# Half of the K tiles of gate and up by Strassen's seven block products, with GpSimd summing the weights

## The chip, the cores and the metric

One NeuronCore of one Trainium2 chip runs the whole program. The metric is device microseconds of one execution. The kernel before took 2407.39 us, the median of 3 runs (2406.78 to 2407.83).

## The reference

The program is a network of three layers over 256 tokens of width 2048, in fp32: two hybrid layers (banded attention, gated linear attention, memory attention), and a third layer with two mixers and a feed forward. Only the feed forward of the third layer matters here:

```
h = rms_norm(x, norm_ffn_pre)                     # (256, 2048)
gate, up = split(h @ w_ffn_in, 2)                 # w_ffn_in: (2048, 2 * 5632)
x = x + rms_norm((silu(gate) * up) @ w_ffn_down, norm_ffn_post)
```

## The kernel before

Weights stay in HBM and stream through SBUF once. A tile of activations is kept as two parts, a high part in the reduced fp32r type and the rest (low); a tile of weights is split in the same way when it arrives. Each product is then three TensorE passes that add up in PSUM: high x high, high x low, low x high (lines 330 to 332). TensorE loads 128 x 128 of the activations as its stationary operand, and 512 columns of the weights stream through: one matmul.

A `Job` is one output of 256 rows by 512 columns (two row tiles t = 0, 1), summed over the K tiles in `order`. `run` cuts each job into parts of two K tiles (1024 columns: one slot of the 41 slots of 128 x 1024 fp32 in SBUF, 512 KB). Per part: one DMA from the SP queue into a slot (`do_load`), one ACT cast into the high slot (line 272) and one VectorE subtraction for the low slot (line 273, `do_split`), then 12 matmuls. `ahead(u)` issues loads up to N_RAW = 4 parts ahead of the splits, and splits as long as at most N_HL = 6 parts are split and not used up; it does this before the matmuls of unit u, so the program order on every engine is fixed when the program is built. All queues work in order.

Work beside the matmuls (evacuations, transposes, attention) is written as generators. `B.clock` is a running estimate of TensorE's time (0.427 ns a column); a generator yields a delay, and `pump`, called after each unit, steps those that are due. The `main` tiles of PSUM (two buffers of two banks) take the jobs in turn; four single banks serve transposes and the rest.

The feed forward has 11 blocks of 512 gate and 512 up columns, in groups of 4, 4 and 3. Each block is two jobs of 16 K tiles. `post_gate2` evacuates the gate (sigmoid on ACT, multiplication on VectorE, line 1533), `post_up2` multiplies the up product into it (line 1539), and the generator `hidden` (after FH = 4000 of the clock) transposes the result (four 128 x 128 transposes at a time, line 377) and splits it into high and low (lines 354 and 355). After each group the down projection runs over its 4 x 512 or 3 x 512 hidden columns as four jobs. The first block is special: it is fed while the norm before it is being finished, and its scale comes late.

Of the kernel before, what the change touches and what calls it, by code (L numbers as in the profile page):

```python
# [9 lines left out]
F32 = mybir.dt.float32  # L10
# [5 lines left out]
P = 128  # L16
# [27 lines left out]
FP = 2500  # L44
FQ = 2500
FS = 8000
FH = 4000
H1 = 10000
H2 = 7500
# [8 lines left out]
class Job:  # L58
# [8 lines left out]

    def __init__(self, kind, w, c0, cn, act, post, pre=None, order=None, k0=0, apart=None):  # L70
# [3 lines left out]
        self.apart = apart or (None, 0, 0)  # L74


class Act:
# [20 lines left out]
class Builder:  # L98
    def __init__(self, ctx, tc, a):
        self.tc, self.nc, self.a = tc, tc.nc, a  # L100
        pool = lambda name, bufs, **kw: ctx.enter_context(tc.tile_pool(name=name, bufs=bufs, **kw))
        self.const = pool("const", 1)
        self.tmp = pool("tmp", 2)
        self.small = pool("small", 4)
        self.psm = pool("psm", 2, space=bass.MemoryType.PSUM)
        self.pss = pool("pss", 4, space=bass.MemoryType.PSUM)
        self.dram = pool("dram", 1, space=bass.MemoryType.DRAM)
        self.free = list(range(N_SLOT))
        self.act = self.const.tile([P, NKT, 2, S], F32R, tag="act", name="act")
# [3 lines left out]
        self.clock = 0.0  # L113
        self.n = 0


# [4 lines left out]
    def alloc(self, n=1, dt=F32):  # L121
        tries = 0
        while len(self.free) < n:
            tries += 1
            assert self.side and tries < 1000, "out of slots"
# [67 lines left out]
        self.tokens[kind] -= 1  # L193

    def pump(self):
        due = [g for g in self.side if self.ready[g] <= self.clock]
        for gen in sorted(due, key=lambda g: self.ready[g])[:2]:
            self.step(gen)
# [14 lines left out]
    def run(self, jobs, loaded_first, split_first):  # L213
# [2 lines left out]
        parts, units = [], []  # L216
        groups = []
        for job in jobs:
            n = NKT if job.kind == "n" else min(1024 // job.cn, 4)
            name, lo, hi = job.apart  # L220
            for j, k in enumerate(range(0, len(job.order), n)):
                key = name if lo <= j < hi else None
                if not (key and groups and groups[-1][0] == key):
                    groups.append((key, []))
                groups[-1][1].append(len(parts))
                parts.append((job, job.order[k:k + n], k))
        for key, mine in groups:
            for ts in ((0,), (1,)) if key else ((0, 1),):
                for i in mine:
                    job, kts, k = parts[i]  # L230
                    units.append((job, i, ts, k == 0 and ts[0] == 0, k + len(kts) == len(job.order), mine[-1]))
        first_use, last_use = {}, {}
        for u, unit in enumerate(units):
# [2 lines left out]
        raws, hls = {}, {}  # L236
        loaded = split = 0

        def pieces(i, n):

            return [slice(k, k + 1) for k in range(n)] if i == 0 else [slice(0, n)]

        def do_load(i):
            job, kts, _ = parts[i]
            (raws[i],) = self.alloc(1)
            n, r0 = len(kts), (job.k0 + kts[0]) * P
            src = job.w[r0:r0 + n * P, job.c0:job.c0 + job.cn].rearrange("(k p) c -> p k c", p=P)
            dst = self.s(raws[i])[:, :n * job.cn].rearrange("p (k c) -> p k c", c=job.cn)
            for ks in pieces(i, n):
                self.load(dst[:, ks], src[:, ks])  # L250
            if i == 0:
                loaded_first()

        def do_split(i):
            job, kts, _ = parts[i]
            n = len(kts) * job.cn
            src = self.s(raws[i])[:, :n]
            if job.kind == "n":
                hls[i] = self.alloc(1, F32R)
                src = src.rearrange("p (k c) -> p k c", c=job.cn)  # L260
                h, l = (self.pair(hls[i], job.cn)[:, :len(kts), j, :] for j in range(2))
            else:
                hls[i] = self.alloc(2, F32R)
                h, l = (self.s(x)[:, :n] for x in hls[i])
            if i == 0:
                for k in range(len(kts)):
                    cs = slice(k * job.cn, (k + 1) * job.cn)
                    self.split_to(h[:, cs], l[:, cs], src[:, cs])
                self.release([raws.pop(i)])
                split_first()  # L270
                return
            nc.scalar.copy(h, src)  # L272
            nc.vector.tensor_tensor(l, src, h.bitcast(F32), ALU.subtract)  # L273
            self.release([raws.pop(i)])

        def room(u):

            _, i, ts, _, _, end = units[u]
            if ts != (0,):
                return len(self.free) > RESERVE  # L280
            if loaded <= end:
                return len(self.free) > 2
            coming = 2 * max(0, end + 1 - split) - sum(r <= end for r in raws)
            return len(self.free) - coming > HOLD

        def ahead(u):

            nonlocal loaded, split
            cap, nraw, reserve, far = N_HL, N_RAW, RESERVE, len(units)
            if len(units[u][2]) == 1:  # L290
                cap, reserve, far = len(parts), 0, u + NEAR
            if u < 8:
                cap, nraw = min(cap, 2 + u), min(nraw, 1 + u)
            while True:
                if loaded < len(parts) and len(raws) < nraw and room(u):
                    do_load(loaded)
                    loaded += 1
                elif split < loaded and len(hls) < cap and len(self.free) > reserve + 1 and first_use[split] <= far:
# [5 lines left out]
        for u, (job, i, ts, first, last, _) in enumerate(units):  # L304
            while split <= i:
                if loaded == split:
                    do_load(loaded)
                    loaded += 1
                do_split(split)
                split += 1  # L310
            if len(ts) == 2:
                ahead(u)
            if first:
                if job.pre:
                    job.pre()
# [5 lines left out]
            for k, kt in enumerate(kts):  # L321
# [3 lines left out]
                st, en = at + k == 0, at + k == len(job.order) - 1  # L325
                if job.kind == "x":
                    for t in ts:
                        o = job.ps[:, t, :job.cn]
                        rows = slice(t * P, t * P + P)
                        nc.tensor.matmul(o, xh[:, rows], h[:, k, :], start=st, stop=False)  # L330
                        nc.tensor.matmul(o, xh[:, rows], l[:, k, :], start=False, stop=False)  # L331
                        nc.tensor.matmul(o, xl[:, rows], h[:, k, :], start=False, stop=en)  # L332
# [13 lines left out]
            if len(ts) == 1:  # L346
                ahead(u)
            self.pump()


    def split_to(self, h, l, src, scale=None):
# [29 lines left out]
def network(ctx, tc, a):  # L381
# [76 lines left out]
    def feeder(act, t, delay, gap=1500):  # L458
        yield delay
        while act.left[t]:  # L460
            act.feed_next(t)
            yield gap


    def halves(ps):
# [96 lines left out]
    def start_late(act, *args):  # L562
        late["gen"] = late_feed(act, *args)
        B.start(late["gen"])
# [927 lines left out]
    def mix_done(ids, t):  # L1492
# [11 lines left out]
        if t == 0:  # L1504
            B.start(feeder(fact, 0, F0, FG))
        else:
            start_late(fact, [f[0], f[1]], x1res, None, lambda: B.release(ids + f["wi"]), False)

    def pre_w2():
        f["wi"] = B.alloc(2)  # L1510
# [30 lines left out]
            B.start(f[("gen", c)])  # L1541
        return post

    def hidden(c, gi):

        yield FH
        if len(f["h"]) <= 2 * c:
            f["h"] += B.alloc(2, F32R)
        for n in range(2):
# [29 lines left out]
    for g, n in enumerate((4, 4, 3)):  # L1579
        for c in range(n):  # L1580
            c0 = 512 * (at + c)
            head = (g, c) == (0, 0)
            jobs.append(Job("x", wf, c0, 512, fact, first_gate if head else post_gate2, apart=("ffn", 0, 8) if head else None))
            jobs.append(Job("x", wf, D_FF + c0, 512, fact, first_up if head else post_up2(c), apart=("ffn", 0, 4) if head else None))
        order, k0 = range(4 * n), 4 * at
# [61 lines left out]
```

## Time and profile before

| | |
|---|---|
| median of 3 runs | 2407.39 us (2406.78 to 2407.83) |
| the profiled execution | 2407.96 us, span 2406.2 us |
| TensorE (PE) busy | 2390.2 us, 12105 matmuls |
| VectorE (DVE) busy | 1476.3 us |
| ScalarE (ACT) busy | 1099.0 us |
| GpSimd (POOL) busy | 400.8 us |

The profile is one execution. PE's busy time is modelled and its matmuls overlap; the distance from one start to the next is what a matmul costs. Busy time of an engine is an average over stages; a stage is read by itself, in a window. In the views, "slot" is any of the SBUF slots, "main_j" the PSUM tile of a job, "bank" one of the single PSUM banks.

### The profile page before, as it was taken

How to read it: one execution, taken by the hardware profiler on the slowest of the kernel's cores; microseconds unless marked ns; L12 is line 12 of the kernel's file. 1: busy time of each engine (PE TensorE's matmuls, PEld its weight loads, DVE VectorE, ACT ScalarE, POOL GpSimd, SP SyncE). 2: the span in 40 equal slices, each digit the busy share in tenths (PEclk: the TensorE clock that was granted, in tenths of full speed). 3: DMA queues.
4: the chain of work that ended last, by engine and by line, in shares of the span. 5: the costliest groups of instructions: out<-in, count | busy, mean ns of one | idle time of the engine just before them, and what ended most of it. 6: DMA issues, size and time to landing. Idle time of an engine off the chain costs nothing. (4 is left out here: it accounts for less than half of the span.)

```text
span 2406.2 us, 31460 instructions
## 1 busy us (share of the span) xinstructions
PE 2390.2 (99%) x12105; PEld 2015.7 (84%) x12105; DVE 1476.3 (61%) x1671; ACT 1099.0 (46%) x1472; POOL 400.8 (17%) x601
## 2 busy tenths in 40 slices
PE   9999999999999999999999999999999999999998
PEld 8888888888888888888888888888888888888886
DVE  6587567666855667766765656657545544554455
ACT  6444445345454553655544544445434423443433
POOL 0330010004400110364764340001000000000000
PEclk9999999999999999999999999999999999999999
DMA  9646567674656674854654666675755655555653
GB/s 327 184 149 184 173 187 262 209 239 133 188 160 186 206 252 156 275 164 125 185 161 146 201 185 194 202 242 186 242 176 180 194 185 193 201 183 177 209 192 131
DMA packets 313911, 464.64 MB, mean 193 GB/s; under 512 B 21961, under 2 KB 161569, under 8 KB 313761
## 3 DMA queue, kind: packets, MB, share of 16 engines
q1 hardware_dynamic: 312528, 459.48, 60.7%
q8 instruction: 95, 1.56, 0.3%
q0 software_dynamic: 640, 2.10, 0.2%
q10 hardware_dynamic: 592, 1.06, 0.1%
q14 instruction: 56, 0.45, 0.1%
HBM read 454.18 MB, written 8.40 MB: 192 GB/s over the span
## 5 line engine op out<-in xcount | busy, mean ns | idle before, releaser
L273 DVE TENSOR_TENSOR slot<-slot,slot 128x1024 fp32r<-128x1024 f32 x810 | 1006.9, 1287 | 190.5 <-ACT slot L272 186.7
L272 ACT CAST slot<-slot 128x1024 fp32r<-128x1024 f32 x810 | 807.8, 1046 | 266.2 <-DVE slot L273 123.6
L339 PE MATMUL main_j<-act,slot 128*128 128x512 f32 x1824 | 651.0, 400 | 0.0
L330 PE MATMUL main_j<-slot,act 128*128 128x512 f32 x1608 | 636.2, 396 | 0.0
L331 PE MATMUL main_j<-slot,act 128*128 128x512 f32 x1608 | 626.4, 390 | 2.8 <-DVE slot L273 2.8
L332 PE MATMUL main_j<-slot,act 128*128 128x512 f32 x1608 | 626.8, 390 | 0.0
L340 PE MATMUL main_j<-act,slot 128*128 128x256 f32 x1824 | 509.9, 280 | 0.0
L339 PEld LDWEIGHTS main_j<-act,slot 128*128 128x128 f32 x1824 | 342.4, 188 | 80.2 <-issue 1.1
L331 PEld LDWEIGHTS main_j<-slot,act 128*128 128x128 f32 x1608 | 302.4, 188 | 63.6 <-DVE slot L273 3.8
L332 PEld LDWEIGHTS main_j<-slot,act 128*128 128x128 f32 x1608 | 301.8, 188 | 63.9
L330 PEld LDWEIGHTS main_j<-slot,act 128*128 128x128 f32 x1608 | 302.2, 188 | 61.3 <-ACT slot L272 0.5
L340 PEld LDWEIGHTS main_j<-act,slot 128*128 128x128 f32 x1824 | 344.1, 189 | 0.8
L330 PE MATMUL main_j<-slot,slot 128*128 128x512 f32 x600 | 236.1, 394 | 0.0
L332 PE MATMUL main_j<-slot,slot 128*128 128x512 f32 x600 | 233.8, 390 | 0.0
L331 PE MATMUL main_j<-slot,slot 128*128 128x512 f32 x600 | 233.6, 389 | 0.0
L447 POOL TENSOR_TENSOR rsl<-rsl,nhalf 128x1 f32<-128x1 f32 x8 | 6.2, 775 | 991.7 <-DVE rsl L446 991.7
L332 PEld LDWEIGHTS main_j<-slot,slot 128*128 128x128 f32 x600 | 112.6, 188 | 23.8
L330 PEld LDWEIGHTS main_j<-slot,slot 128*128 128x128 f32 x600 | 112.7, 188 | 23.0
L331 PEld LDWEIGHTS main_j<-slot,slot 128*128 128x128 f32 x600 | 112.8, 188 | 22.5
L674 POOL TENSOR_TENSOR slot<-slot 128x128 f32<-128x128 f32 x144 | 79.2, 581 | 191.9 <-PE main_j L339 92.8
L354 ACT CAST slot<-bank 128x512 fp32r<-128x512 f32 (+1 forms) x30 | 15.9, 529 | 177.7 <-PE bank L377 170.7
L813 POOL TENSOR_TENSOR slot<-slot,tz 128x512 f32<-128x512 f32 x20 | 25.8, 1290 | 397.8 <-DVE tz L812 397.8
(193 smaller groups left out, 1738.4 us busy)
## 6 DMA issues: line engine op xcount, KB each, us to landing
slot<-in_w_in_dram SPq DMA_DIRECT2D x384, 512.0 KB, 4.0
slot<-in_w_ffn_in_dram SPq DMA_DIRECT2D x176, 512.0 KB, 4.6
slot<-in_w_ffn_down_dram SPq DMA_DIRECT2D x88, 512.0 KB, 4.6
slot<-in_w_out_dram SPq DMA_DIRECT2D x64, 512.0 KB, 4.7
slot<-in_w_o_dram SPq DMA_DIRECT2D x32, 512.0 KB, 4.5
slot<-in_w_mem_kv_dram SPq DMA_DIRECT2D x31, 512.0 KB, 5.9
slot<-in_w_up_b_dram SPq DMA_DIRECT2D x16, 512.0 KB, 4.6
slot<-in_w_up_a_dram SPq DMA_DIRECT2D x16, 512.0 KB, 4.4
```

The source lines that it names most:

```text
L272: nc.scalar.copy(h, src)
L273: nc.vector.tensor_tensor(l, src, h.bitcast(F32), ALU.subtract)
L330: nc.tensor.matmul(o, xh[:, rows], h[:, k, :], start=st, stop=False)
L331: nc.tensor.matmul(o, xh[:, rows], l[:, k, :], start=False, stop=False)
L332: nc.tensor.matmul(o, xl[:, rows], h[:, k, :], start=False, stop=en)
L339: nc.tensor.matmul(job.ps[:, f, :], h[:, k, fs], xs, start=st, stop=False)
L340: nc.tensor.matmul(job.ps[:, f, :S], l[:, k, fs], xh, start=False, stop=en)
L354: nc.scalar.copy(h, src)
L447: G.tensor_tensor(out, out, nhalf[:, :n], ALU.pow)
L674: G.tensor_tensor(view(E[:, l, :]), view(bt), ref, ALU.subtract)
L813: G.tensor_tensor(y, y, tz, ALU.mult)
```

## The change

The first block stays. In each of the other ten, K tiles 0 to 7 of gate and up go on as two ordinary jobs, which leave their sums open in PSUM. K tiles 8 to 15 are taken in two quads of four. In a quad, the two row tiles, the two halves of the K tiles and gate against up form a 2 x 2 by 2 x 2 block product, and a `Shared` job makes it from seven products of (128 x 256) by (256 x 512), in Winograd's form of Strassen's scheme, in the order c, d, a, T1, T2, T4, T3. Each product is a part of its own, with its own cast and subtraction, and 2 K tiles x 3 passes = 6 matmuls.

Four products need sums of weights: as soon as the raw tiles have landed, GpSimd adds up and gate in place (`do_load`), and then, when tile a has been split, makes three more (`sums`), each in place of a raw tile whose own split is done. The sums of activations (`combos_of`) are made once for each quad and kept in slots. Four of the products accumulate in the four single banks, which the job takes all; the others go into the open sums in `main`. At the end of a block the results are put together in slots: copies on ACT, four additions on VectorE, four on GpSimd. `hidden` then does sigmoid and multiplications from the slots, after FG2 = 5000 of the clock, and the transposes after FH more; `pump` holds still for 4000 after a block. Up to 8 split parts may be kept around the products.

```diff
+    names = ("c", "d", "a", "T1", "T2", "T4", "T3")
...
+            elif ("b", i) in raws:
+                b = raws[("b", i)]
+                add(b, raws[i], b)
...
+        def sums(job, name, q):
+
+            at = lambda x: index[id(job), x, q]
+            if name == "a":
+                a, d, c = (raws[at(x)] for x in "adc")
+                t1 = raws[("b", at("a"))]
+                add(d, t1, d)
+                add(c, d, c)
+                add(a, d, a, ALU.subtract)
...
+            if job.kind == "s":
+                name, q = kts
+                at = lambda x: index[id(job), x, q]
+                key = {"T1": ("b", at("a")), "T2": at("d"), "T3": at("a"), "T4": at("c")}.get(name, i)
+                hls[i] = self.alloc(2, F32R)
+                self.split_to(*(self.s(x) for x in hls[i]), self.s(raws[key]))
+                sums(job, name, q)
+                if name[0] == "T":
+                    self.release([raws.pop(key)])
+                return
...
+            if job.kind == "s" or u + 1 < len(units) and units[u + 1][0].kind == "s":
+                cap += 2
...
+                wanted = need[split - 1] if split else 0
+                if loaded < len(loads) and loaded - wanted < nraw and room(u):
...
+        if (name, q) == ("c", 0):
+            nc.scalar.copy(gb[:, 1], ps_b[:, 1])
+        ka, kb = job.quads[q][:2], job.quads[q][2:]
+        x = {"c": (kb, 0), "a": (ka, 0), "T4": (kb, 1)}.get(name)
+        o = {"c": ps_a[:, 0], "T4": ps_a[:, 1], "d": ps_b[:, 0]}.get(name)
...
+            self.three(o, xh, xl, hl[0][:, k, :], hl[1][:, k, :], fresh and k == 0, last and k == 1)
+        self.clock += 2 * 3 * 512 * 0.427
+        if not last:
+            return
+        V, A, G = nc.vector, nc.scalar, nc.gpsimd
+        if name == "c":
+            A.copy(ga[:, 0], o)
+        elif name == "d":
+            A.copy(gb[:, 0], o)
+        elif name == "a":
+            A.copy(m1, o)
+            G.tensor_tensor(ga[:, 0], ga[:, 0], m1, ALU.add)
+        elif name == "T2":
+            V.tensor_tensor(u, o, m1, ALU.add)
+            V.tensor_tensor(w, job.m["T1"], u, ALU.add)
+            G.tensor_tensor(gb[:, 0], gb[:, 0], w, ALU.subtract)
+        elif name == "T4":
+            A.copy(ga[:, 1], o)
+        elif name == "T3":
+            V.tensor_tensor(v, o, u, ALU.add)
+            V.tensor_tensor(u, o, w, ALU.add)
+            G.tensor_tensor(ga[:, 1], ga[:, 1], v, ALU.add)
+            G.tensor_tensor(gb[:, 1], gb[:, 1], u, ALU.subtract)
+            self.held, self.quiet = False, self.clock + 4000
+            self.release(job.tmp)
+            job.post(*job.out)
...
+    def hidden(c, gi, ui=None):
+
+        yield FG2 if ui else FH
+        if ui:
+            for t in range(2):
+                sg, g, r = B.ttile([P, 512], "tz"), vt(gi)[:, t, :], rs2[:, t:t + 1]
+                A.activation(sg, g, AF.Sigmoid, scale=r)
+                V.scalar_tensor_tensor(g, g, r, sg, ALU.mult, ALU.mult)
+                V.scalar_tensor_tensor(g, vt(ui)[:, t, :], r, g, ALU.mult, ALU.mult)
+            B.release([ui])
+            yield FH
...
+            if not head:
+                std = range(8)
+                gate = Job("x", wf, c0, 512, fact, lambda ps: None, order=std, open=(0, 1))
+                up = Job("x", wf, D_FF + c0, 512, fact, lambda ps: None, order=std, open=(0,))
+                jobs.extend([gate, up, Shared(gate, up, QUADS, fact, fcombos, post_both(c))])
+                continue
```

## Rows read from the trace of the kernel before

**Rows 1.** The page: busy time of the engines; the granted TensorE clock by slices.
```profile
span 2406.2 us, 31460 instructions
PE 2390.2 (99%) x12105; PEld 2015.7 (84%) x12105; DVE 1476.3 (61%) x1671; ACT 1099.0 (46%) x1472; POOL 400.8 (17%) x601
...
PEclk9999999999999999999999999999999999999999
```

**Rows 2.** Chain of waits, in the feed forward: start, us, step.
```profile
2026.59 0.44 PE bank L377 x4
...
2071.08 0.44 PE bank L377 x4
...
2115.56 0.44 PE bank L377 x4
```

**Rows 3.** Busy time of each engine in two stretches of one block.
```profile
core 0: us, PE busy (x) PEld busy (x) DVE busy (x) ACT busy (x) POOL busy (x), PEclk, DMA share, GB/s
2026.59:2071.08 44.49, 44.49 (x203) 36.83 (x201) 22.73 (x22) 17.94 (x20) 0.00 (x0) 1.00 0.56 189
2247.09:2291.58 44.49, 44.49 (x202) 36.82 (x201) 22.72 (x22) 17.94 (x20) 0.00 (x0) 1.00 0.56 189
```

**Rows 4.** Groups of instructions, one block, 2026.59 to 2071.08.
```profile
L273 DVE TENSOR_TENSOR slot<-slot,slot 128x1024 fp32r<-128x1024 f32 x16 | 18.5, 1219 | 0.7 <-ACT slot L272 0.7
L272 ACT CAST slot<-slot 128x1024 fp32r<-128x1024 f32 x16 | 15.7, 1053 | 2.8 <-PE main_j L332 1.7 <-issue 1.1
...
L355 DVE TENSOR_TENSOR slot<-bank,slot 128x512 fp32r<-128x512 f32 x2 | 1.4, 692 | 3.9 <-ACT slot L354 3.9
...
L354 ACT CAST slot<-bank 128x512 fp32r<-128x512 f32 x2 | 1.2, 587 | 14.6 <-PE bank L377 14.6
```

**Rows 5.** Instructions in order of time, GpSimd, 882 to 895 us: start, us.
```profile
883.86 2.39 POOL L1150 TENSOR_TENSOR slot<-slot,slot 128x1024 f32<-128x1024 f32 x1 [33.98 <-DMA slot<-in_norm_mix_pre_dram]
886.33 2.40 POOL L1151 TENSOR_TENSOR slot<-slot,slot 128x1024 f32<-128x1024 f32 x1
888.68 2.40 POOL L1150 TENSOR_TENSOR slot<-slot,slot 128x1024 f32<-128x1024 f32 x1
891.16 2.42 POOL L1151 TENSOR_TENSOR slot<-slot,slot 128x1024 f32<-128x1024 f32 x1
```

**Rows 6.** The same stretch, VectorE.
```profile
889.29 0.69 DVE L1074 SCALAR_TENSOR_TENSOR slot<-slot,main_j 128x512 f32<-128x512 f32 x1 [9.96 <-PE main_j L332]
...
890.62 0.67 DVE L1074 SCALAR_TENSOR_TENSOR slot<-slot,main_j 128x512 f32<-128x512 f32 x1
...
891.94 4.99 DVE L273 TENSOR_TENSOR slot<-slot,slot 128x1024 fp32r<-128x1024 f32 x3
```

**Rows 7.** In order of time, GpSimd and VectorE, 620 to 633 us.
```profile
622.71 2.42 POOL L720 TENSOR_TENSOR slot<-slot,slot 128x1024 f32<-128x1024 f32 x1
625.07 3.13 POOL L718 TENSOR_TENSOR slot<-slot,slot 128x896 f32<-128x896 f32 x1
628.14 3.42 POOL L720 TENSOR_TENSOR slot<-slot,slot 128x1024 f32<-128x1024 f32 x1
...
623.82 8.83 DVE L273 TENSOR_TENSOR slot<-slot,slot 128x1024 fp32r<-128x1024 f32 x3 [4.62 <-ACT slot L272]
```

**Rows 8.** GpSimd at 128x512: line 1243 (min/median/max ns), then 960 to 973 us.
```profile
L1243 POOL TENSOR_TENSOR slot<-slot,om x4: 1040/1041/1253, 998.7 to 1144.6; 128x512 f32<-128x512 f32 x4
...
960.34 13.84 POOL L1121 TENSOR_TENSOR slot<-slot,slot 128x512 f32<-128x512 f32 x8 [21.21 <-DMA slot<-in_ln_b_dram]
959.74 7.57 DVE L1113 SCALAR_TENSOR_TENSOR slot<-slot,mvt,slot 128x512 f32<-128x512 f32 x5
969.04 6.22 DVE L273 TENSOR_TENSOR slot<-slot,slot 128x1024 fp32r<-128x1024 f32 x3 [1.73 <-ACT slot L272]
```

**Rows 9.** Line 1481, duration ns min/median/max.
```profile
L1481 DVE SCALAR_TENSOR_TENSOR slot<-slot,rsl,slot x16: 746/747/1786, 1649.8 to 2401.4; 128x512 f32<-128x512 f32 x16
```

**Rows 10.** DMA issues by tensor: count, KB each, median us to landing.
```profile
slot<-in_w_ffn_in_dram SPq DMA_DIRECT2D x176, 512.0 KB, 4.6
```

**Rows 11.** Busy time by stretches with TensorE idle (columns as in rows 3).
```profile
1120.00:1140.00 20.00, 18.30 (x111) 15.90 (x110) 16.24 (x34) 13.97 (x24) 7.17 (x9) 1.00 0.31 86
2398.00:2406.00 8.00, 0.00 (x0) 0.00 (x0) 3.42 (x7) 0.40 (x2) 0.55 (x1) 0.59 0.36 132
```

More of the change, by code (lines that the diff above doesn't have):

```diff
@@ L46 @@
 FS = 8000
+FG2 = 5000
 FH = 4000
@@ L112, in __init__ @@
         self.tokens = {"att": N_ATT, "lin": N_LIN}
-        self.clock = 0.0
+        self.clock, self.quiet, self.held = 0.0, 0.0, False
         self.n = 0
@@ L124, in alloc @@
             tries += 1
-            assert self.side and tries < 1000, "out of slots"
+            assert self.side and tries < 1000 and not self.held, ("out of slots", n, len(self.free), self.held, self.dbg())
             self.step_all()
@@ L218, in run @@
         for job in jobs:
+            if job.kind == "s":
+                for q in range(len(job.quads)):
+                    for name in job.names:
+                        groups.append((None, [len(parts)]))
+                        parts.append((job, (name, q), 0))
+                continue
             n = NKT if job.kind == "n" else min(1024 // job.cn, 4)
@@ L237, in run, with add @@
         loaded = split = 0
+        loads, need, index = [], [], {}
+        for i, (job, kts, _) in enumerate(parts):
+            if job.kind != "s":
+                loads.append((i, job, kts))
+            else:
+                name, q = kts
+                index[id(job), name, q] = i
+                quad = job.quads[q]
+                if name in "cd":
+                    loads.append((i, job.a if name == "c" else job.b, quad[2:]))
+                elif name == "a":
+                    loads.append((("b", i), job.b, quad[:2]))
+                    loads.append((i, job.a, quad[:2]))
+            need.append(len(loads))
         def pieces(i, n):
             return [slice(k, k + 1) for k in range(n)] if i == 0 else [slice(0, n)]
+        def add(out, x, y, op=ALU.add):
+            nc.gpsimd.tensor_tensor(self.s(out), self.s(x), self.s(y), op)
         def do_load(i):
-            job, kts, _ = parts[i]
+            i, job, kts = loads[i]
             (raws[i],) = self.alloc(1)
@@ L280, in room @@
                 return len(self.free) > RESERVE
-            if loaded <= end:
+            if loaded < need[end]:
                 return len(self.free) > 2
-            coming = 2 * max(0, end + 1 - split) - sum(r <= end for r in raws)
+            coming = 2 * max(0, end + 1 - split) - sum(type(r) is int and r <= end for r in raws)
             return len(self.free) - coming > HOLD
@@ L294, in ahead @@
             while True:
-                if loaded < len(parts) and len(raws) < nraw and room(u):
+                wanted = need[split - 1] if split else 0
+                if loaded < len(loads) and loaded - wanted < nraw and room(u):
                     do_load(loaded)
                     loaded += 1
-                elif split < loaded and len(hls) < cap and len(self.free) > reserve + 1 and first_use[split] <= far:
+                elif split < len(parts) and need[split] <= loaded and len(hls) < cap and len(self.free) > reserve + 1 and first_use[split] <= far:
                     do_split(split)
@@ L304, in run @@
         for u, (job, i, ts, first, last, _) in enumerate(units):
+            self.dbg = lambda: (jobs.index(job), len(jobs), parts[i][1], "raws", len(raws), "hls", len(hls), "loaded", loaded, "split", split, "i", i)
             while split <= i:
-                if loaded == split:
+                while loaded < need[split]:
                     do_load(loaded)
@@ L312, in run @@
                 ahead(u)
+            if job.kind == "s":
+                self.shared(job, *parts[i][1], [self.s(x).rearrange("p (k c) -> p k c", c=512) for x in hls[i]])
+                self.release(hls.pop(i))
+                self.pump()
+                continue
             if first:
@@ L327, in run @@
                     for t in ts:
-                        o = job.ps[:, t, :job.cn]
                         rows = slice(t * P, t * P + P)
-                        nc.tensor.matmul(o, xh[:, rows], h[:, k, :], start=st, stop=False)
-                        nc.tensor.matmul(o, xh[:, rows], l[:, k, :], start=False, stop=False)
-                        nc.tensor.matmul(o, xl[:, rows], h[:, k, :], start=False, stop=en)
+                        self.three(job.ps[:, t, :job.cn], xh[:, rows], xl[:, rows], h[:, k, :], l[:, k, :],
+                                   st, en and t not in job.open)
                 elif job.kind == "n":
@@ L348, in run, with three, shared @@
             self.pump()
+    def three(self, o, xh, xl, h, l, start, stop):
+        nc = self.nc
+        nc.tensor.matmul(o, xh, h, start=start, stop=False)
+        nc.tensor.matmul(o, xh, l, start=False, stop=False)
+        nc.tensor.matmul(o, xl, h, start=False, stop=stop)
+    def shared(self, job, name, q, hl):
+        nc, last = self.nc, q == len(job.quads) - 1
+        ps_a, ps_b = job.a.ps, job.b.ps
+        if (name, q) == ("c", 0):
+            for quad in job.quads:
+                for kt in quad:
+                    job.act.ensure(kt, (0, 1))
+                    job.act.get(kt)
+            job.combos(0)
+            self.held = True
+            job.m = dict(zip(("a", "T1", "T2", "T3"), (self.bank() for _ in range(4))))
+            job.out = self.alloc(2)
+            job.tmp = self.alloc(2)
+        ga, gb, u, w = (self.s(x).rearrange("p (t c) -> p t c", t=2) for x in job.out + job.tmp)
+        m1, u, w, v = u[:, 0], u[:, 1], w[:, 0], w[:, 1]
+        if (name, q) == ("c", 0):
+            nc.scalar.copy(gb[:, 1], ps_b[:, 1])
+        ka, kb = job.quads[q][:2], job.quads[q][2:]
+        x = {"c": (kb, 0), "a": (ka, 0), "T4": (kb, 1)}.get(name)
+        o = {"c": ps_a[:, 0], "T4": ps_a[:, 1], "d": ps_b[:, 0]}.get(name)
+        fresh = o is None and q == 0
+        if o is None:
+            o = job.m[name]
+        for k in range(2):
+            if x:
+                act = job.act.get(x[0][k])
+                xh, xl = (act[:, j, x[1] * P:(x[1] + 1) * P] for j in range(2))
+            else:
+                n = ("T1", "T2", "T3", "d").index(name)
+                xh, xl = (y[:, n, k, :] for y in job.combos(q))
+            self.three(o, xh, xl, hl[0][:, k, :], hl[1][:, k, :], fresh and k == 0, last and k == 1)
+        self.clock += 2 * 3 * 512 * 0.427
+        if not last:
+            return
+        V, A, G = nc.vector, nc.scalar, nc.gpsimd
[3 more added lines that the diff above has]
+            A.copy(gb[:, 0], o)
+        elif name == "a":
+            A.copy(m1, o)
[14 more added lines that the diff above has]
+            job.post(*job.out)
@@ L1506, in mix_done, with done @@
         else:
-            start_late(fact, [f[0], f[1]], x1res, None, lambda: B.release(ids + f["wi"]), False)
+            def done():
+                B.release(ids + f["wi"])
+                f["make"] = make_fcombos()
+                B.start(f["make"])
+            start_late(fact, [f[0], f[1]], x1res, None, done, False)
     def pre_w2():
@@ L1542, in post_up2, with make_fcombos, fcombos, post_both @@
         return post
-    def hidden(c, gi):
-        yield FH
+    QUADS = [(8, 9, 10, 11), (12, 13, 14, 15)]
+    def make_fcombos():
+        for quad in QUADS:
+            f.setdefault("combos", []).append(combos_of(lambda k: B.act[:, k:k + 2], quad))
+            yield 3000
+    def fcombos(q):
+        if f["make"] in B.side:
+            B.drain([f["make"]])
+        return parted(f["combos"][q])
+    def post_both(c):
+        def post(gi, ui):
+            f[("gen", c)] = hidden(c, gi, ui)
+            B.start(f[("gen", c)])
+            f["units"] = f.get("units", 1) + 1
+            if f["units"] * 512 == D_FF:
+                B.release(sum(f["combos"], []))
+        return post
+    def hidden(c, gi, ui=None):
[8 more added lines that the diff above has]
+            yield FH
         if len(f["h"]) <= 2 * c:
```

32 lines of the change are left out of this document (30 added, 2 removed).

## The prediction

> **What bounds the kernel now.** I read the page's busy shares first, then the mean clock, then the stages. TensorE (PE) is busy 2390.2 of 2406.2 us, VectorE (DVE) 61%, ScalarE (ACT) 46%, GpSimd (POOL) 17%, and the granted clock is at its upper level, 2.4 GHz, in every slice [rows 1]. The span stands 1.8 us below the profiled execution's 2407.96 us, which is 0.6 us above the median of the three runs, 2407.39; sums below are made against 2407.96, and what they add is taken to hold for the median too.
>
> The change touches only the feed forward. In the chain of waits one block of 512 gate and 512 up columns starts where the four transposes of the block before stand: 2026.59, 2071.08, 2115.56, so 44.49 us a block [rows 2]. In it TensorE has no idle time at all, and VectorE is busy 22.73, ScalarE 17.94, GpSimd 0 us [rows 3]. A block is 16 K tiles x 2 row tiles x 2 outputs x 3 passes = 192 matmuls of 512 columns and 8 transposes; four transposes take 0.44 us in the chain, so (44.49 - 0.88) / 192 = 0.227 us a matmul. The feed forward is bound by the number of matmuls, and any one removed is 0.227 us, as long as the split weights arrive in time. Ten of the eleven blocks change; the first stays.
>
> **TensorE's gain.** In each of the ten, K tiles 0 to 7 keep 96 matmuls; K tiles 8 to 15 go as two quads of 7 products x 2 K tiles x 3 passes = 84 instead of 96. So 12 x 0.227 = 2.72 us less: 41.77 us a block if nothing is late, 27.2 us in all.
>
> **What VectorE and GpSimd get in exchange, per block.** Now: 16 splits (an ACT cast, 1.05 us, and a DVE subtraction, 16 in 18.5 us, so 1.15 each) [rows 4]. After: 8 splits for K tiles 0 to 7 and 14 for the products, 22. New on GpSimd: 8 sums of 128x1024. These have near relatives in the trace: L1150 and L1151, two slots in and one out, 2.40 us each, 2.43 from start to start [rows 5].
>
> The important question is whether these sums run beside the subtractions. At 888.68 to 891.3 us, VectorE's L1074 (one input in SBUF, the other in PSUM) takes 0.67 to 0.69 us while GpSimd works: no loss. But the L273 subtractions from 891.94, which read two slots, come to 4.99 us for three, 1.5 more than 3 x 1.15: the first is held until the sum ends at 893.58 [rows 5, 6]. Both slow where they meet for longer: a GpSimd 128x1024 product that took 2.42 us at 622.71 takes 3.42 at 628.14, and three L273 in that stretch take 8.83 us instead of 3.45 [rows 7]. The two engines take turns, one operation each: a sum and a subtraction together cost 3.4 us, nearly 2.43 + 1.15. The same with other shapes: eight GpSimd 128x512 sums take 13.84 us (1.73 each, alone 1.04) while two-slot DVE operations run beside them [rows 8], and the two-slot DVE operation L1481 goes from 0.746 to 1.786 us at worst [rows 9].
>
> The Trainium skill, page "SBUF — State Buffer", section "Who interferes with whom", states the rule: a VectorE instruction with two SBUF inputs and a GpSimd instruction that reads SBUF exclude one another for the whole instruction, while a VectorE instruction with at most one SBUF input is free. Rows 5 to 7 bear both halves out, but for a tenth or two of overlap: by the rule a pair would cost 2.40 + 1.22 = 3.62 us, by the rows 3.4, so eight pairs 29.0 against 27.4.
>
> So I treat two-slot DVE work and GpSimd work as one resource ("the pair") and add up a block's need of it:
> - 8 sums, each with a subtraction: 8 x 3.42 = 27.4 us.
> - 14 further subtractions: 14 x 1.15 = 16.1.
> - GpSimd's 4 combinations of 128x512 at the end: 1.04 alone [rows 8], 4.2.
> - The hidden step's 4 SCALAR_TENSOR_TENSOR, which now read gate, up and sigmoid from slots, where they read PSUM before: 0.746 each [rows 9], 3.0.
>
> That is 50.7 us that can't overlap. VectorE has six more operations with one input in PSUM (4 combinations, 2 splits of the hidden values) at 0.69 [rows 4]: 4.1 us, nothing if they fall under a GpSimd sum, all of it if not. I take a little over half, as GpSimd is busy about half of the block, and a block becomes 53 us, between 50.7 and 54.8. PE needs 41.8. The pair is the new bound; ACT is not (22 casts x 1.05, 5 copies, 2 sigmoids and 2 casts of 0.6 to 0.7: 29 us).
>
> **Why it isn't 10 x 53.** Splits run up to six parts ahead of TensorE, eight at the products. The first changed block of each group (three of the ten) comes after work with fewer splits than VectorE can do, so some five are done when it starts, and no combinations of a block before stand in its way. It needs 27.4 + 9 x 1.15 = 37.8 us of the pair, inside TensorE's 41.8: I take 41.8. It ends without a lead, and the other seven pay in full. 3 x 41.8 + 7 x 53 = 496.4 us against 10 x 44.49 = 444.9: +51.5.
>
> **Ends of groups.** The down projection needs a split only every 12 x 0.227 = 2.72 us, so VectorE recovers at once; its first matmul waits for one subtraction, 3 x 1.2 = 3.6 us. The hidden step now holds a sigmoid and two multiplications that are put off by 5 us of the builder's clock before the 4 us that it had. In the third group (12 K tiles) its result is wanted after 8 K tiles, 48 x 0.227 = 10.9 us, so its second transpose, cast (0.59) and split (0.69) [rows 4] come right before their reader: 2 to 3 us. Together +6.
>
> **At nothing.** The sums of x (once, 10 GpSimd operations up to 128x512, at most 1.3 us each: 13 us) fall in the first block and the start of the second, where GpSimd does nothing and VectorE is idle half the time [rows 3]; uncovered, up to 13. Loads: the same 16 of 512 KB, landing in 4.6 us [rows 10], up to four ahead, in a longer block; uncovered, one landing a group, 14 us. On ACT the five PSUM copies stand behind casts that are already ahead; the next gate's first matmul needs the copy of T4, and T3's six matmuls (1.36 us) cover its 0.6; uncovered, under 1 us a block. All eight PSUM banks are held during the products, so transposes wait until the next block; they need 1 us of PE and are late nowhere else.
>
> **Sum.** 2407.96 + 51.5 + 6 = 2465.5, so 2466 us, for the median 2465.
>
> **Rivals.**
> - *A, the forecast*: the pair bounds seven of ten blocks, 2466. Own range 2443 (50.7 a block, nothing lost at the ends: 3 x 41.8 + 7 x 50.7 - 444.9 = +35) to 2495 (54.8 and the three first blocks at 44, +71, the ends and 10 of the items at nothing).
> - *B, faster*: the matmul stays the bound and 27 us come off: 2381. For it: VectorE alone needs 22 x 1.15 + 3.0 + 4.1 = 32 us of 41.8, GpSimd 8 x 2.43 + 4.2 = 24, each with room; sums can be made during the first eight K tiles, where VectorE has slack. It decides at the price of a sum with its subtraction: 8p + 16.1 + 4.2 + 3.0 = 41.8 gives p = 2.3, no more than a sum by itself, and no time lost against before would need p near 2.7. Rows 5 to 7 say 3.42, in several places.
> - *C, slower still*: TensorE now works 9.5 us of each 17 in the products, in bursts of six matmuls. If the clock falls to 1.2 GHz there, the products take 84 x 0.454 = 38.1 and the block 38.1 + 96 x 0.227 + 0.9 = 60.8: 3 x 41.8 + 7 x 60.8 - 444.9 = +106, 2520. In the trace the clock stays up where PE is idle 1.7 of 20 us, and falls (0.59 in the mean) only in the last 8 us, in which PE does nothing [rows 11]; nothing in between is shown. The Trainium skill, page "TensorE: Matmul & The Clock Gate", section "HAM oscillation — how this bites in real kernels", tells of kernels whose waits between bursts bring the clock down again and again; no run here shows it.
> - *D, in between*: p is near 2.7 and the time stays about the same, 2403 to 2412.
>
> **Chances.** A 0.70, B 0.13, C 0.12, D 0.05. Differences under 0.2% (5 us) can't be told from none here. B and a little of D are faster: 0.14; D's middle the same: 0.03; A and C slower: 0.83. The range 2420 to 2530 leaves out B and D, and a tail above C.
>
> **What would show it.** In a block of the changed kernel: blocks 53 us apart within a group, the first of each near 42; TensorE idle before product matmuls, ended by DVE subtractions; L273 well above its 1.22 us in the mean (towards 2) and the new GpSimd sums at 3.4 rather than 2.4; GpSimd and two-slot DVE work together filling the block. It is wrong if TensorE is still without idle time in the feed forward (B), or if the granted clock there is visibly under 1.00 (C).

## The result, and the profile after

The changed kernel takes 2486.11 us (median of 4 runs, 2484.74 to 2486.96), the kernel before beside it 2407.09: 79.0 us slower, a ratio of 1.0327 with the interval 1.0309 to 1.0345. The forecast was 2466, slower, with a range of 2420 to 2530.

The page of the changed kernel, busy time and clock, beside [rows 1]:

```profile
span 2483.0 us, 31698 instructions
PE 2398.2 (97%) x11985; PEld 2011.7 (81%) x11985; DVE 1752.3 (71%) x1775; ACT 1190.7 (48%) x1584; POOL 737.5 (30%) x731
...
PEclk9999999999999999999999999999999999999989
```

There are 120 matmuls fewer (12105 - 11985), as counted, yet TensorE is busy 8 us longer and stands still for 85 us where it stood still for 16. The page's clock line hides what happens: its slices are 62 us long. Windows show it. The first row is the first changed block of the second group, which has no transposes (they come later); the other two rows are the two stretches behind it, each from transposes to transposes (columns as in [rows 3]):

```profile
1952.20:1993.00 40.80, 40.80 (x181) 33.78 (x180) 35.58 (x20) 19.30 (x21) 21.87 (x8) 1.00 0.36 113
2012.62:2066.87 54.25, 45.39 (x188) 36.69 (x188) 50.04 (x33) 26.71 (x31) 32.47 (x12) 0.94 0.48 156
2066.87:2121.15 54.28, 45.65 (x189) 36.88 (x189) 49.79 (x33) 26.70 (x31) 31.98 (x12) 0.94 0.48 155
```

The first block has no idle time in TensorE and takes 40.8 us. The others take 54.3 instead of 44.49; TensorE is idle 9 us of each, VectorE busy 50 and GpSimd 32, where it was 0. VectorE's 50 is not 50 us of work, as the groups of instructions from 1700 us on show (L498 is the subtraction of the products, L345 that of the ordinary parts, L273 before; L290 is the new sum; to the right of the bar busy us and mean ns):

```profile
L498 DVE TENSOR_TENSOR slot<-slot,slot 128x1024 fp32r<-128x1024 f32 x142 | 298.5, 2138 | 19.5 <-ACT slot L497 9.5 <-issue 7.8 <-PE bank L433 0.9
L290 POOL TENSOR_TENSOR slot<-slot,slot 128x1024 f32<-128x1024 f32 x80 | 249.2, 3130 | 266.7 <-DMA slot<-in_w_ffn_in_dram 156.9 <-issue 67.3 <-DVE slot L498 24.2
L345 DVE TENSOR_TENSOR slot<-slot,slot 128x1024 fp32r<-128x1024 f32 x168 | 228.0, 1393 | 39.9 <-ACT slot L344 37.8 <-POOL slot L488 2.0
```

The same subtraction that took 1.219 us [rows 4] takes 2.138 us among the sums, and a sum 3.13 instead of 2.40 [rows 5]. The two engines take turns; while either waits, it counts as busy. In order of time, where they meet, in one block:

```profile
2072.93 9.88 POOL L290 TENSOR_TENSOR slot<-slot,slot 128x1024 f32<-128x1024 f32 x3
...
2075.31 10.85 DVE L498 TENSOR_TENSOR slot<-slot,slot 128x1024 fp32r<-128x1024 f32 x5 [0.25 <-ACT slot L497]
```

Three sums in 9.88 us are 3.29 each. Five subtractions in 10.85 us would be 5.75 at 1.15. Taking the starts and ends of all instructions from 2066.87 to 2121.15, one of the two engines is at work (or in the other's way) for 52.4 of the 54.3 us.

What TensorE waited for from 1700 us on (us in all, times, longest); before, this list is empty for the same stretch:

```profile
PE bank L520 <- DVE slot L1741: 36.1, 19, 5.8
PE main_j L431 <- ACT slot L452: 31.4, 8, 5.8
PE main_j L431 <- ACT slot L472: 1.4, 1, 1.4
PE main_j L433 <- DVE slot L498: 0.9, 1, 0.9
```

Nearly none of it is put down to the subtractions (0.9 us). The waits turn up at two places that stand behind them in program order: the hidden step's transposes (L520), which need VectorE's last multiplication (L1741), and the d product's first matmul, which needs ACT's copy of up's second row tile out of the same PSUM tile (L452). That copy stands on ACT behind casts that wait for GpSimd:

```profile
2076.24 1.05 ACT L497 CAST slot<-slot 128x1024 fp32r<-128x1024 f32 x1 [0.96 <-POOL slot L290]
2079.55 1.99 ACT L497 CAST slot<-slot 128x1024 fp32r<-128x1024 f32 x2 [2.25 <-POOL slot L290]
2081.44 0.58 ACT L452 COPY slot<-main_j 128x512 f32<-128x512 f32 x1
```

And behind such a wait the clock is at its lower level, 1.2 GHz: the matmuls that follow stand 0.43 us apart, not 0.227.

```profile
2082.07 0.76 PE L431 MATMUL main_j<-slot,slot 128*128 128x512 f32 x1 [4.25 <-ACT slot L452]
2082.63 0.63 PE L432 MATMUL main_j<-slot,slot 128*128 128x512 f32 x1
2083.06 0.63 PE L433 MATMUL main_j<-slot,slot 128*128 128x512 f32 x1
```

From 1714 us to the end, 115 matmuls go so, 24.9 us more than at 0.227 each, and TensorE's gaps add up to 70.2. With 27.2 us of matmuls gone that makes +68 of the 76.8 us by which the span grew. Most of the rest lies in the waits too: a gap is counted from the modelled end of a matmul, 0.39 us after its start, but the next would have started after 0.227. From start to start the waits cost about 76 us. Nothing is lost ahead of the first changed block, which starts 0.8 us earlier than in the kernel before.

### The profile page after: what moved, and what is told of

It reads as the page before. It is cut to its first block, busy times and chain, and to the rows that moved or that the text cites. A ratio compares the mean times of both kernels' runs of the same rounds, so it can differ in the third digit from the quotient of the medians.

```text
span 2483.0 us, 31698 instructions
## 1 busy us (share of the span) xinstructions
PE 2398.2 (97%) x11985; PEld 2011.7 (81%) x11985; DVE 1752.3 (71%) x1775; ACT 1190.7 (48%) x1584; POOL 737.5 (30%) x731
## 5 line engine op out<-in xcount | busy, mean ns | idle before, releaser
L345 DVE TENSOR_TENSOR slot<-slot,slot 128x1024 fp32r<-128x1024 f32 x730 | 950.0, 1338 | 219.2 <-ACT slot L344 212.7
L344 ACT CAST slot<-slot 128x1024 fp32r<-128x1024 f32 x730 | 734.6, 1047 | 290.6 <-PE main_j L433 113.0
L431 PE MATMUL main_j<-slot,act 128*128 128x512 f32 x1368 | 547.1, 400 | 1.6 <-ACT slot L472 1.4
L432 PE MATMUL main_j<-slot,act 128*128 128x512 f32 x1368 | 536.6, 392 | 1.6 <-DVE slot L345 1.6
L433 PE MATMUL main_j<-slot,act 128*128 128x512 f32 x1368 | 536.2, 392 | 0.0
L290 POOL TENSOR_TENSOR slot<-slot,slot 128x1024 f32<-128x1024 f32 x80 | 249.2, 3130 | 266.7 <-DMA slot<-in_w_ffn_in_dram 156.9
L498 DVE TENSOR_TENSOR slot<-slot,slot 128x1024 fp32r<-128x1024 f32 (+1 forms) x162 | 311.6, 1959 | 20.9 <-ACT slot L497 10.9
L431 PEld LDWEIGHTS main_j<-slot,act 128*128 128x128 f32 x1368 | 259.6, 190 | 55.0 <-ACT slot L472 2.4
L433 PEld LDWEIGHTS main_j<-slot,act 128*128 128x128 f32 x1368 | 259.0, 189 | 55.5
L432 PEld LDWEIGHTS main_j<-slot,act 128*128 128x128 f32 x1368 | 259.5, 190 | 53.7 <-DVE slot L345 2.8
L431 PE MATMUL main_j<-slot,slot 128*128 128x512 f32 x640 | 257.0, 402 | 31.6 <-ACT slot L452 31.4
L433 PE MATMUL main_j<-slot,slot 128*128 128x512 f32 x640 | 253.8, 397 | 1.0 <-DVE slot L498 0.9
L432 PE MATMUL main_j<-slot,slot 128*128 128x512 f32 x640 | 253.4, 396 | 0.0
L497 ACT CAST slot<-slot 128x1024 fp32r<-128x1024 f32 (+1 forms) x162 | 158.6, 997 | 162.9 <-POOL slot L290 78.4
L431 PEld LDWEIGHTS main_j<-slot,slot 128*128 128x128 f32 x640 | 122.5, 191 | 60.4 <-ACT slot L452 34.8
L433 PEld LDWEIGHTS main_j<-slot,slot 128*128 128x128 f32 x640 | 122.5, 191 | 28.5 <-DVE slot L498 2.4
L432 PEld LDWEIGHTS main_j<-slot,slot 128*128 128x128 f32 x640 | 122.8, 192 | 24.3
```

The costliest lines, as they stand in the source:

```text
L290: nc.gpsimd.tensor_tensor(self.s(out), self.s(x), self.s(y), op)
L431: nc.tensor.matmul(o, xh, h, start=start, stop=False)
L432: nc.tensor.matmul(o, xh, l, start=False, stop=False)
L433: nc.tensor.matmul(o, xl, h, start=False, stop=stop)
```

## The experiments

The profile allows two readings. Theory 1: GpSimd's sums and VectorE's two-slot operations exclude each other and together need more than TensorE's 41.8 us a block; the places at which TensorE waits are only where the lack shows. Theory 2: the places are the cost, an early copy and late transposes in queues that work in order. The clock by itself is a third.

**Without the sums.**

```diff
         def add(out, x, y, op=ALU.add):
-            nc.gpsimd.tensor_tensor(self.s(out), self.s(x), self.s(y), op)
+            pass
```

> Leaves out GpSimd's eight sums of weights per block; the four products that need sums take unsummed tiles, all splits, matmuls and loads stay. Theory 1 (VectorE's two-slot subtractions and GpSimd's sums take turns and fill a block): the pair's need falls to 22 x 1.15 + 4.2 + 3.0 = 32.5 us a block, with the PSUM operations 36.6, under TensorE's 41.8; TensorE is the bound again and the time is 2381 to 2392 us. Theory 2 (the 22 splits by themselves, with the copy and transposes placed behind them in order, are what TensorE waits for): the waits stay, above 2440. Theory 3 (half-speed clock by itself, in the bursts of six matmuls): the granted clock stays under 1.00 in the blocks and the time above 2420.

Measured: 2394.36 us, ratio 0.9946 (0.9932 to 0.9961): 92 us faster than the changed kernel, for 80 sums of 2.4 us on an engine that did nothing in these blocks before the change. The subtractions among the products are back:

```profile
L498 DVE TENSOR_TENSOR slot<-slot,slot 128x1024 fp32r<-128x1024 f32 x142 | 169.7, 1236 | 48.2 <-ACT slot L497 24.1 <-PE bank L433 11.4 <-PE main_j L433 6.0
```

and the blocks are 42.9 us apart. The time is 2 us above the expected 2381 to 2392: TensorE still waits 0.8 us for the copy in seven blocks. The clock is 0.997 in the mean. In the bursts of six matmuls it stays up; in the whole feed forward it falls once, at 2324 us, in a pair of waits of 1.6 and 1.1 us at the last transposes. Theory 1 stands; theory 2 alone (above 2440) and the clock alone (above 2420) fall.

**The copy made late,** together with the copy behind d.

```diff
-        if (name, q) == ("c", 0):
-            nc.scalar.copy(gb[:, 1], ps_b[:, 1])
...
-            A.copy(gb[:, 0], o)
+            A.copy(gb, ps_b)
```

> The copy of up's second row tile out of PSUM, which the d product's first matmul waited for (31.4 us in all), is taken out of its place ahead of the products and made together with the copy behind d, as one copy of both banks. Theory 1 (GpSimd and VectorE, which together are busy 52.4 of a block's 54.3 us, bound the block): the wait turns up later, in front of other products or the transposes; at most the 1.9 us a block that the two are idle come off, 2468 to 2486 us. Theory 2 (in-order placement of the copy is the cost): the 31 us go, and some of the half-speed stretches behind them, 2435 to 2455.

Measured: 2488.87 us (2486.33 to 2492.8), against 2486.11: nothing gained. The 31 us at the copy are gone from TensorE's waits and stand elsewhere:

```profile
PE bank L518 <- DVE slot L1739: 25.8, 16, 4.0
PE main_j L431 <- ACT slot L470: 21.7, 8, 3.3
PE bank L432 <- DVE slot L496: 16.7, 15, 1.7
```

Now TensorE waits for the subtractions themselves (L496, 16.7 us), for another copy and for the transposes. That is what a bound by throughput would look like. Theory 1's expectation (2468 to 2486) was even a little too low.

**The sums on VectorE.**

```diff
-            nc.gpsimd.tensor_tensor(self.s(out), self.s(x), self.s(y), op)
+            nc.vector.tensor_tensor(self.s(out), self.s(x), self.s(y), op)
```

> The eight sums of weights per block go to VectorE, in the same places of the program. Theory 1: a sum there costs about 1.15 us and nothing takes turns but the four small combinations: VectorE needs 30 x 1.15 + 3.0 + 4.1 = 41.6 us, with GpSimd's 4.2 up to 45.8, against TensorE's 41.8: later blocks 43 to 46, the time 2390 to 2412 us, about that of the kernel before. Theory 2 (the chain from sum to cast to subtraction, and what stands in order behind it): VectorE now has both in one queue and gets no earlier through; above 2450.

Measured: 2426.27 us, ratio 1.0083 (1.0066 to 1.0099): 60 us faster than with the same sums on the idle engine, though VectorE has eight operations more in each block.

```profile
L498 DVE TENSOR_TENSOR slot<-slot,slot 128x1024 fp32r<-128x1024 f32 x142 | 166.6, 1218 | 18.2 <-ACT slot L497 12.6 <-PE bank L433 5.0 <-PE main_j L433 0.6
L290 DVE TENSOR_TENSOR slot<-slot,slot 128x1024 f32<-128x1024 f32 x80 | 97.3, 1247 | 4.9 <-DMA slot<-in_w_ffn_in_dram 4.2
```

A sum costs 1.25 us there and the subtractions 1.22. The time lies 14 us above theory 1's 2390 to 2412, and below theory 2's 2450. The two later blocks of the first group take the 42.9 us of the run without sums, but the five of the other groups take 48.1 to 49.7, where 43 to 46 was expected: in four of them TensorE waited 3.3 us for the early copy, and in all five 0.9 to 2.7 us at the transposes. So here the places seem to cost something as well; this run doesn't separate them from VectorE's load.

**One quad.** K tiles 12 to 15 alone; 0 to 11 ordinary.

```diff
-    QUADS = [(8, 9, 10, 11), (12, 13, 14, 15)]
+    QUADS = [(12, 13, 14, 15)]
...
-                std = range(8)
+                std = range(12)
```

> Only K tiles 12 to 15 go as a quad; 0 to 11 stay ordinary. TensorE: 186 matmuls, 43.1 us a block with its transposes. Theory 1: the pair needs 4 x 3.42 + 15 x 1.15 + 4.2 + 3.0 = 38.1 us, 42.2 with the PSUM operations, under TensorE's 43.1: the block is TensorE's, 10 x 1.36 us come off the kernel before, 2394 us, with a few us for the group's ends and the copy up to 2404: no slower than before, where two quads are 79 slower. Theory 2 (each quad costs its copy, its transposes behind VectorE and the ends, a fixed price per block): most of the loss stays, since a block still has one copy and one late hidden step: 2440 to 2480.

Measured: 2411.77 us, ratio 1.0018 (1.0009 to 1.0027). Half of the change costs 4 us where all of it costs 79: a threshold, not a price for each quad. Theory 1's sign was wrong, though (2394 to 2404 expected): blocks are 45.05 us apart, of which 1.6 are the wait for the copy, in seven blocks:

```profile
PE main_j L431 <- ACT slot L452: 11.2, 7, 1.6
PE bank L520 <- DVE slot L1741: 1.5, 2, 1.1
```

**GpSimd only writes.** Each sum becomes two fills of the same tile.

```diff
-            nc.gpsimd.tensor_tensor(self.s(out), self.s(x), self.s(y), op)
+            for _ in range(2):
+                nc.gpsimd.memset(self.s(out), 0.5)
```

> Each of GpSimd's eight sums per block is replaced by two fills of the same 128x1024 tile with a constant, so the output differs; GpSimd now only writes SBUF, and the chain sum, cast, subtraction keeps its places. No row shows such a fill; 64x256 took 0.30 us, so I guess 1 to 2.4 us for two. Theory 1 (what costs is that GpSimd's reads and VectorE's two-slot operations take turns): the subtractions are back near 1.22 us, the blocks near 43, the time 2392 to 2410. Rival (GpSimd's chain is long by itself, whatever it reads): casts and subtractions wait for it as before, 2440 to 2487 us, with the subtractions at 1.22 too but TensorE idle.

Measured: 2394.44 us, the same as without the sums (2394.36).

```profile
L499 DVE TENSOR_TENSOR slot<-slot,slot 128x1024 fp32r<-128x1024 f32 x142 | 170.8, 1237 | 55.2 <-ACT slot L498 30.7 <-PE bank L434 11.4 <-PE main_j L434 6.0
L291 POOL MEMSET slot<- 128x1024 f32 x160 | 150.1, 956 | 277.5 <-DMA slot<-in_w_ffn_in_dram 147.3 <-DVE slot L499 107.4 <-ACT slot L345 6.6
```

GpSimd works 2 x 0.956 = 1.9 us in place of each 2.4 us sum, in the same chain before cast and subtraction, and the subtractions stay at 1.237 us. So neither GpSimd's length nor the chain is the cost (a fifth shorter though it is here): it is that its operations read SBUF while VectorE reads two slots. The Trainium skill, page "SBUF — State Buffer", section "Who interferes with whom", says this: a VectorE instruction with two SBUF inputs contends with a GpSimd instruction that reads SBUF, not with one that only writes it. This run agrees.

**One quad with the late copy**, and the same **with the sums on VectorE** (the edits above, put together).

> One quad, as in the run before with K tiles 12 to 15 alone, and up's copy out of PSUM made late, with d's. Theory 1: with one quad the pair (38 to 42 us) no longer bounds the block, so the 1.6 us that TensorE waited for the copy in 7 blocks, nothing with two quads, now count: 7 x 1.6 = 11 off 2411.8, 2398 to 2403 us, faster than before by 0.2 to 0.4%. Rival (the pair is the bound here too): the wait turns up elsewhere and the time stays at 2408 to 2413.

> One quad, late copy, and the four sums on VectorE. VectorE's need is 23 x 1.15 + 3.0 + 4.1 = 33.6 us, 37.8 with GpSimd's combinations, against TensorE's 43.1. Theory 1: TensorE bounds the block with and without it: the same as one quad with the sums on GpSimd, 2397 to 2403. Rival (the pair still bounds one quad on GpSimd): this one is faster than that by 5 us or more.

Measured: 2399.66 us, ratio 0.9968 (0.9956 to 0.9981), and 2398.44 us, ratio 0.9964 (0.9951 to 0.9976). Both beat the kernel before. The late copy, worth nothing with two quads, is worth 12.1 us with one, and TensorE's waits are nearly gone:

```profile
PE bank L518 <- DVE slot L1739: 2.9, 2, 1.8
PE main_j L431 <- ACT slot L495: 0.7, 3, 0.2
```

Blocks are 43.1 us apart in both, TensorE's 186 matmuls and 8 transposes. That sums on GpSimd or on VectorE differ by 1 us shows that the pair does not bound a block with one quad. It also answers what the fills left open: the full-length sum in the chain before cast and subtraction, slower on GpSimd, costs next to nothing with one quad.

**Two quads, everything on VectorE**, with the late copy; the four combinations at the end of a block too.

```diff
-            G.tensor_tensor(gb[:, 0], gb[:, 0], w, ALU.subtract)
+            V.tensor_tensor(gb[:, 0], gb[:, 0], w, ALU.subtract)
...
```

> Two quads, all eight sums and the four combinations on VectorE, late copy: nothing takes turns, GpSimd has no work in the blocks. VectorE needs 30 x 1.15 + 3.0 + 4.1 + 2.8 = 44.4 us a block, TensorE 41.8. Theory 1: VectorE alone is the bound: later blocks 44.4 to 46, the first of a group near 41, against 48.2 with the combinations on GpSimd and the early copy: 2396 to 2412 us. Rival (the chain from sum to cast to subtraction, in one queue, bounds it): 2420 or more.

Measured: 2413.93 us, ratio 1.0029 (1.0017 to 1.0040), 2 us above the expected range. With nothing to take turns with, VectorE is busy 92.4 of 100 us. The seven later blocks come to 45.1 us in the mean, where VectorE's sum gave 44.4 and TensorE's 41.8; that VectorE by itself is now the bound is argued from this, not shown by a run of its own. It is 12 us less than with the sums alone on VectorE, but the late copy and the moved combinations came together, so their shares are open:

```profile
2000.00:2100.00 100.00, 92.42 (x393) 74.82 (x392) 92.36 (x93) 55.17 (x62) 0.00 (x0) 0.95 0.53 182
```

**Two quads where there is slack.** First in the first changed block of each group only, on GpSimd; then in every other block, on VectorE; late copy in both.

```diff
+                two = c == (1 if g == 0 else 0)
+                std = range(8 if two else 12)
...
+                jobs.extend([gate, up, Shared(gate, up, QUADS if two else QUADS[1:], fact,
+                                              fcombos if two else lambda q: fcombos(q + 1), post_both(c))])
```

> Two quads in the first changed block of each group only, one quad in the other seven, sums and combinations on GpSimd, late copy. Theory 1: the first block of a group starts with splits already made and nothing left over from a block before, and the changed kernel ran it in 40.7 us with two quads; so 3 x 1.36 = 4.1 us come off the one-quad kernel with the late copy (2399.7), 2395 to 2397. Rival (the block behind it then starts without a lead and pays): 2399 to 2410.

> Two quads in every other block (six of ten, the first of each group among them), one quad in the rest; sums and combinations on VectorE, late copy. VectorE needs 44.4 us in a block of two and 36.4 in a block of one, 80.8 for both, against TensorE's 84.9. Theory 1 (throughput of VectorE bounds): 6 x 1.36 = 8.2 us come off the one-quad kernel with sums on VectorE (2398.4), 2390 to 2393. Rival (splits run too few parts ahead for a block to use the slack of the next): the blocks of two that aren't the first of a group stay near 45, 2396 to 2404.

Measured: 2413.85 us, ratio 1.0028 (1.0018 to 1.0037), and 2397.68 us, ratio 0.9961 (0.9948 to 0.9973). The first missed by 17 us, in the direction of the rival and 4 us beyond its range too. In the second and third groups the block of two itself is short, but the block behind it ends 48.0 and 46.4 us after it, where the one-quad kernel has 43.1: TensorE waits there 1.64 and 1.19 us at the transposes, which need VectorE, and in the second group the clock falls as well. That the block starts without a lead, and that one quad on GpSimd (38 to 42 us of the pair by the sum) leaves too little slack to win it back, is argued. In the first group the first block itself also waited, 3.3 us for a copy:

```profile
PE bank L518 <- DVE slot L1739: 9.8, 6, 3.2
PE main_j L431 <- ACT slot L470: 3.3, 1, 3.3
```

The second is level with one quad throughout (2398.44), and inside the rival's range, but not in the rival's way. The blocks of two that are not the first of a group take 41.8, 43.2 and 42.4 us, not 45: there VectorE's need was averaged over blocks nearly as theory 1 said. At the last product of the last group the profiled execution is 5.3 us ahead of the one-quad kernel (2312.6 against 2317.9), of the 8.2 us of matmuls saved. It loses 5.6 us behind that, at the last transposes and in the half-speed matmuls after them:

```profile
PE bank L518 <- DVE slot L1739: 6.9, 4, 4.9
```

So what used up the gain is mostly the end of the last group, where TensorE waits for VectorE's last multiplications behind a block of two. Whether ending the group with a block of one keeps the gain was not run.

## Why the prediction was right, step by step

- *The bound.* Right. The pair's need of a block was put at 53 us, 50.7 to 54.8; the seven later blocks came out at 53.85 in the mean, from the last product of one to that of the next (376.9 us for the seven; 371 were forecast). The price of a sum with its subtraction, 3.42 us from [rows 7], was 3.2 to 3.4 from one sum's start to the next. In the block taken apart above, the two engines are at work for 52.4 us and neither for 1.9, which the sum had not; that the number agrees within 1 us is in part luck.
- *The first block of each group.* Right in two of three: 40.8 us in the second and third group, where 41.8 was taken (the 1 us is transposes, which fall into the next block). In the first group it took 45.5: TensorE waited 1.7 us for the early copy of up and 1.4 for another copy (L472).
- *Where it would be seen.* Wrong in part. The forecast looked for TensorE idle "before product matmuls, ended by DVE subtractions". Only 0.9 us was so. With in-order queues the lack showed at an ACT copy and at the transposes; that this was only the place, the late copy showed for the copy; for the transposes it is argued.
- *At nothing: the copies.* "Under 1 us a block" was named for the next gate's wait for T4; the early copy of up was passed over as standing behind casts that are already ahead. They were not ahead: they waited for the sums. TensorE waited 1.7 to 5.8 us for it in eight blocks: a cost as a place, nothing as a cause with two quads, and 1.6 a block as a cause with one, the difference between 0.2% slower and 0.3% faster (2411.77 against 2399.66).
- *Ends of groups.* This is the mis-sized term: +6 was forecast, about +17 came (2.1, 5.9 and 8.8 us, from the last product of a group to the last matmul of its down projection, against the same stretches before). VectorE comes out of the last block with a backlog, and the hidden step's transposes wait for it, 5.8 us in the third group; half-speed matmuls follow.
- *The sum.* +58 forecast: +60 for the seven later blocks, -8 for the three first, +6 at the ends. The trace gives +65.5, -4.4 and +16.8; with 1.1 less ahead of the first changed block and behind the last matmul, that is the 76.8 by which the span grew. All three terms came out too low, the ends by most; the range covered it.
- *Rivals.* B's time (2381) needs the sums to cost nothing in turns; without their reads the kernel takes 2394, so B had the direction of what would follow, and is 13 us too low. C came true in a part: the granted clock is 0.90 to 0.94 in the five later blocks looked at. The prediction had named a clock visibly under 1.00 as a sign that it was wrong, and that sign appeared. But the clock falls in or behind waits, from two of 1.0 to 1.4 us close together up to single ones of 5.8, not in the bursts by themselves, and it rises again: it follows from the waits that A forecast, and the sign could not tell A from C. (C's "9.5 us of each 17" doesn't come out of the forecast: 53 less 21.8 and 0.9 leaves 15.2 us for a quad. C's time doesn't use it.) How much of the 25 us would be left at full clock can't be said: TensorE would then have waited longer for the pair, as in the kernel with the late copy, where waits and slow matmuls lie elsewhere and the time is the same. This stays open.

## What to carry to other kernels

Before work goes to an idle engine, ask what it shares with the busy one: here an engine at 0% in the stage could not take 24 us of 54 without taking them from VectorE, and the same sums were 60 us cheaper on the engine that looked loaded. Add up a stage's need of a shared resource over both engines, and compare it with the bound before trading matmuls for it; half of the trade, one quad, fitted under that bound and, with the copy made late, gained 0.3 to 0.4%. And where a wait is listed shows the place, not the cause: moving a 31 us wait bought nothing until the bound behind it was gone.

## What the runs showed of the hardware that was not expected

- GpSimd fills of 128x1024 (0.956 us each) beside VectorE's two-slot subtractions leave them at 1.237 us, where GpSimd sums of the same tiles bring them to 2.138.
- Waits of TensorE of 3 to 6 us in the middle of a busy stage were followed by matmuls 0.43 us apart, at 1.2 GHz, for several us; the single waits of 0.8 us in the run without sums, and of 1.6 us in the run with one quad, were not.
- The same waits did not always do the same: two of 1.64 and 1.19 us, close together, at the same place of the program brought the clock down in the second group of the run with two quads in each group's first block, and not in the third. The block behind took 48.0 us in the one case and 46.4 in the other.
